# Turning the first two FFN tiles by DMA transposes of 16-bit halves instead of by TensorE

## The chip, the core and the metric

The kernel runs on one core of a Trainium2 chip. The metric is device time in microseconds (us) of one execution; less is better. The engines that matter are TensorE (PE: matmuls, with its weight loads as PEld), VectorE (DVE), ScalarE (ACT), GpSimd (POOL) and SyncE (SP), which issues the DMAs. Each engine works through its own queue of instructions in order, and semaphores make one engine wait for another. On-chip memory is SBUF; matmuls write into PSUM, which has eight banks of 128 partitions by 512 float32 values.

## The reference

One decoder layer on `x` of 256 positions by 1024 features, all float32. A mixer part (attention and a short convolution in parallel, with gates) is followed by a residual and a LayerNorm, and then by a feed-forward part (FFN) with a second residual and LayerNorm. Cut to what matters here:

```python
x = layer_norm(DEEPNORM_ALPHA * x + mix, ln1_g[l], ln1_b[l])
u = causal_dwconv(x @ w_up[l], conv_w_ffn[l])          # w_up: 1024 x 5632, three taps over positions
f = (silu(u[..., :D_FF]) * u[..., D_FF:]) @ w_down[l]  # D_FF = 2816
x = layer_norm(DEEPNORM_ALPHA * x + f, ln2_g[l], ln2_b[l])
```

The convolution runs over positions, channel by channel. It is therefore convenient to hold `x @ w_up` with the channels on the 128 partitions and the 256 positions along the free axis.

## The kernel before

**Arithmetic.** Every float32 operand of a matmul is split into a high part, rounded by a ScalarE copy to TensorE's reduced format, and a low part, which VectorE gets by subtraction. A product is the sum of high times high, high times low and low times high: three passes (`mm3`, L322), or, where the weights are the stationary side, one pass over high and low of the activations at once (`cols_wide`, L337) and one of the low weights (`cols_narrow`, L344).

**Weights.** All weights lie packed in HBM in chunks of up to 1 MB, in the order of `plan()` (L60). A chunk holds two units. SP loads the chunks in order into three rotating buffers (`raw`, `issue_dma`, L172), so the chunk after the next two can be loaded only when both units of the oldest have been split. `split_h` (L199) issues the chunk two ahead, and then makes a unit's high part on ScalarE; `split_l` (L210) makes its low part on VectorE. ScalarE's copy waits for its chunk's DMA, and everything behind it in ScalarE's queue waits with it.

**FFN.** The hidden width is cut into 22 tiles of 128 channels, each with a gate half and a value half. For tiles 2 to 21, two units (`g`, `v`) give the tile with channels on partitions in a pair of PSUM banks. Four stages follow, each with a ScalarE and a VectorE part (`FFN`, L938): stage 0 adds the two halves of the bank pair into SBUF, stage 1 applies the three convolution taps, stage 2 the silu and the product, stage 3 splits the finished tile `f` into high and low. Then `down(i)` (L978) multiplies tile i with two halves of a `w_dn` row unit, twelve passes into four PSUM banks.

**Tiles 0 and 1** are different. Their weights (`up0`) are the moving side, because `x1` for the second half of the positions comes late. `up0_rows(t)` (L950) computes 128 positions by 512 channels for t = 0 and t = 1: positions on partitions, the wrong way round. ScalarE copies the two results to SBUF (L962, L966), and eight TensorE transposes (`up0_T`, L970) turn them into two PSUM banks, one for each tile. Between the two results stand four weight splits (L963).

**Order.** The order of the work is written out by hand in `seq` (L1007): for each tile the steps `g` and `v`, and a `d` step (one `down`) for the tile three before. After step k's matmuls, `slot(k, stages)` (L1019) puts beside them: the ScalarE parts of one or two waiting tile stages, the high splits up to six steps ahead, the low splits up to five ahead, and then the VectorE parts of those stages. `take` picks the stages from `pending`, oldest first, not two of one tile. Beside a `v` step stage 0 of its tile comes first. After step 0 the transposes are issued (L1046), and the stages 1 to 3 of tiles 0 and 1 join `pending`. So tile 0's stages 1, 2 and 3 stand beside steps 0, 1 and 2, and its `down` is step 4.

The kernel already turns attention probabilities by DMA (`probs_halves`, `probs_T`, `probs_words`, L460 to L470): VectorE takes 32-bit words apart into two planes of 16-bit halves, SP issues a DMA transpose of 12 blocks of 128 by 128 halves, and ScalarE puts the words together again.

## Time and profile before

| | |
|---|---|
| time, median of 3 runs | 361.46 us (361.29 to 361.51) |
| profiled execution | 361.25 us, of which 359.5 us from the first to the last instruction |
| TensorE matmul busy | 352.1 us, 98% of the span |
| VectorE busy | 302.2 us, 84% |
| ScalarE busy | 238.9 us, 66% |
| DMA moved | 71.20 MB, mean 198 GB/s |
| mean granted TensorE clock | 0.995 |

Times in the profile count from the start of the span. A row of a group gives the line of the kernel, the engine, the operation, output and inputs by their names in the program, the shapes, the count, the busy time in us with the mean of one in ns, and the idle time of the engine just before with what ended it. A row of the timeline gives start and length in us. The chain of waits goes back from the last instruction, at each step to what released it; since matmuls are pipelined, its pieces of TensorE show the pace and not the full length of one matmul. A DMA's time to landing runs from its issue on SP to its completion.

### The profile page before, as it was taken

The page shows a single profiled execution, that of the slowest core. Times are in us where ns is not written, and L with a number is a line of the kernel's source. Part 1 is how long each engine was busy: PE and PEld are TensorE (multiplying, and loading weights), DVE is VectorE, ACT ScalarE, POOL GpSimd, SP SyncE. Part 2 cuts the span into 40 slices and gives each one's busy share as a digit, 9 for nine tenths or more (in the row PEclk, how much of TensorE's full clock was granted, in tenths as well). Part 3 has the DMA queues.
Part 4 walks back from the last instruction along what each step waited for, and adds up shares of the span by engine and source line. Part 5 has one row for each costly group of instructions (what it writes and reads, how often), then busy time and mean ns, then how long its engine had stood idle before and what let it go on. Part 6 is the DMA issues. An engine that isn't in the chain of part 4 may idle for free.

```text
span 359.5 us, 5201 instructions
## 1 busy us (share of the span) xinstructions
PE 352.1 (98%) x1915; PEld 304.3 (85%) x1915; DVE 302.2 (84%) x522; ACT 238.9 (66%) x415; POOL 22.1 (6%) x49
## 2 busy tenths in 40 slices
PE   9999999999999999999999999999999999999993
PEld 8888889888887888888888888888888888988883
DVE  4687987999888989989769789997869696999875
ACT  4586768699999976652557466766647475677800
POOL 2000001100000112310000000000000000000110
PEclk9999999999999999999999999999999999999998
DMA  8979663753955765679061736538091735663002
GB/s 284 323 263 338 221 240 122 246 168 129 261 170 174 301 228 190 216 297 339 15 233 74 277 129 224 202 148 343 19 338 59 295 127 225 233 232 120 1 33 85
DMA packets 17370, 71.20 MB, mean 198 GB/s; under 512 B 7488, under 2 KB 8000, under 8 KB 10304
## 3 DMA queue, kind: packets, MB, share of 16 engines
q1 hardware_dynamic: 16768, 68.77, 53.2%
q0 software_dynamic: 576, 2.10, 2.0%
q8 instruction: 15, 0.25, 0.3%
q14 instruction: 11, 0.09, 0.1%
HBM read 68.24 MB, written 1.05 MB: 193 GB/s over the span
## 4 chain that ended last, share of the span: by engine, by line
PE 78%; ACT 10%; DVE 7%; issue 3%; POOLq 0%; POOL 0%; DVEq 0%; ACTq 0%
PE pb L342 20%; PE pb L349 11%; PE d L324 5%; PE d L325 5%; PE d L326 4%; PE y L342 4%; PE k L614 3%; PE v L614 3%; ACT wh L203 3%; PE q L614 3%; DVE wl L213 2%; PE y L349 2%; PE o L324 2%; PE o L326 2%; PE o L325 2%
## 5 line engine op out<-in xcount | busy, mean ns | idle before, releaser
L213 DVE TENSOR_TENSOR wl<-raw,wh 128x1024 fp32r<-128x1024 f32 x99 | 121.4, 1230 | 25.3 <-ACT wh L203 25.1
L203 ACT ACTIVATE wh<-raw 128x1024 fp32r<-128x1024 f32 x99 | 103.8, 1055 | 30.5 <-DMA raw<-in_wpack 30.3
L342 PE MATMUL pb<-x1T,wh 128*128 128x512 f32 x320 | 76.2, 390 | 0.0
L342 PEld LDWEIGHTS pb<-x1T,wh 128*128 128x128 f32 x320 | 59.7, 188 | 12.1
L349 PEld LDWEIGHTS pb<-x1T,wl 128*128 128x128 f32 x320 | 41.0, 191 | 1.6
L349 PE MATMUL pb<-x1T,wl 128*128 128x256 f32 x320 | 41.5, 283 | 0.0
L342 PE MATMUL g<-xT,wh 128*128 128x512 f32 x128 | 31.6, 393 | 0.6 <-DVE gs L733 0.6
L236 DVE TENSOR_TENSOR wl<-raw,wh 128x1024 fp32r<-128x1024 f32 (+2 forms) x29 | 27.0, 974 | 5.0 <-ACT wh L235 4.8
L235 ACT ACTIVATE wh<-raw 128x1024 fp32r<-128x1024 f32 (+2 forms) x29 | 23.4, 853 | 9.8 <-DMA raw<-in_wpack 5.8
L324 PE MATMUL d<-wh,f 128*128 128x512 f32 x76 | 29.8, 392 | 0.0
L325 PE MATMUL d<-wl,f 128*128 128x512 f32 x76 | 29.8, 391 | 0.0
L326 PE MATMUL d<-wh,f 128*128 128x512 f32 x76 | 29.6, 389 | 0.0
L342 PEld LDWEIGHTS g<-xT,wh 128*128 128x128 f32 x128 | 23.2, 188 | 5.5 <-PE av L486 0.8
L902 ACT ACTIVATE fb<-pb 128x512 f32<-128x512 f32 x20 | 11.9, 595 | 13.1 <-PE pb L349 13.1
L920 DVE SCALAR_TENSOR_TENSOR fc<-fb,consts,fc 128x254 f32<-128x254 f32 x40 | 19.3, 483 | 1.4
L918 DVE SCALAR_TENSOR_TENSOR fc<-fb,consts,fc 128x255 f32<-128x255 f32 x40 | 19.2, 480 | 0.0
L912 ACT ACTIVATE fc<-fb,consts 128x256 f32<-128x256 f32 x40 | 18.0, 499 | 0.6 <-DVE fb L906 0.6
L349 PEld LDWEIGHTS g<-xT,wl 128*128 128x128 f32 x128 | 16.4, 191 | 0.7
L326 PEld LDWEIGHTS d<-wh,f 128*128 128x128 f32 x76 | 14.3, 188 | 3.1
L349 PE MATMUL g<-xT,wl 128*128 128x256 f32 x128 | 16.6, 282 | 0.0
L324 PEld LDWEIGHTS d<-wh,f 128*128 128x128 f32 x76 | 14.3, 189 | 2.6
L325 PEld LDWEIGHTS d<-wl,f 128*128 128x128 f32 x76 | 14.3, 189 | 2.4
(210 smaller groups left out, 595.4 us busy)
## 6 DMA issues: line engine op xcount, KB each, us to landing
raw<-in_wpack SPq DMA_DIRECT2D x55, 1024.0 KB, 5.0
raw<-in_wpack SPq DMA_DIRECT2D x6, 896.0 KB, 6.1
xr<-in_x SPq DMA_DIRECT2D x1, 1024.0 KB, 7.0
ln<-in_ln_g POOLq DMA_DIRECT2D x2, 512.0 KB, 5.7
ln<-in_ln_b POOLq DMA_DIRECT2D x2, 512.0 KB, 6.3
raw<-in_wpack SPq DMA_DIRECT2D x2, 384.0 KB, 4.2
raw<-in_wpack SPq DMA_DIRECT2D x2, 256.0 KB, 3.1
raw<-in_wpack SPq DMA_DIRECT2D x1, 512.0 KB, 6.0
```

The lines of the kernel that those rows point to most:

```text
L203: nc.scalar.activation(units[u]["h"], raw_of(u), AF.Copy)
L213: nc.vector.tensor_tensor(units[u]["l"], raw_of(u), units[u]["h"].bitcast(F32), op=ALU.subtract)
L235: nc.scalar.activation(h, src, AF.Copy)
L236: (eng or nc.vector).tensor_tensor(l, src, h.bitcast(F32), op=ALU.subtract)
L324: nc.tensor.matmul(o, ah, bh, start=start, stop=False)
L325: nc.tensor.matmul(o, ah, bl, start=False, stop=False)
L326: nc.tensor.matmul(o, al, bh, start=False, stop=stop)
L342: nc.tensor.matmul(bank, un["h"][:, k, n0:n0 + P], b[:, k].rearrange("p a s -> p (a s)"), start=k == 0, stop=False)
L349: nc.tensor.matmul(bank[:, 0:S], un["l"][:, k, n0:n0 + P], b[:, k, 0], start=False, stop=k == nk - 1)
L614: nc.tensor.matmul(banks[m][t], (xl if p == 2 else xh)[:, k, t * P:(t + 1) * P], wl if p == 1 else wh, start=k == 0 and p == 0, stop=k == ...
L918: nc.vector.scalar_tensor_tensor(c[:, 1:S], pb[:, a * S:a * S + S - 1], w_ffn(1, j), c[:, 1:S], op0=ALU.mult, op1=ALU.add)
L920: nc.vector.scalar_tensor_tensor(c[:, 2:S], pb[:, a * S:a * S + S - 2], w_ffn(0, j), c[:, 2:S], op0=ALU.mult, op1=ALU.add)
```

## The change

The rows of tiles 0 and 1 are no longer turned by TensorE. For each t, ScalarE copies the PSUM bank to SBUF as two planes of 16-bit halves (`up0_halves`: 128 partitions by 1024 halves), and SP issues a DMA transpose of these eight blocks. Before the first of these, the chunk that `split(u0 + 4)` would issue is issued. Beside step 2 instead of step 0, ScalarE puts the halves together again as words in SBUF (`up0_words`, two copies of 512 halves for each tile), and stages 1 to 3 of the two tiles join `pending` there. Two PSUM banks are no longer taken for tiles 0 and 1, and stages read these tiles from SBUF. The `down` steps come one tile later in `seq`, four behind instead of three, and the `w_dn` chunks one pair of chunks later in `plan()`.

```diff
@@ plan()
-        d = c - 1
+        d = c - 2
@@ layer_kernel
-    rows = {}
+    up16 = big.tile([P, 2, 2, 1024], U16, tag="x", name="up16")
...
-        rr = scratch([P, 512], f"up0r_{t}")
-        rows[t] = rr
-        return bank, rr
-
-    b0, r0 = up0_rows(0)
+        return bank
+
+    def up0_halves(t, bank):
+        nc.scalar.activation(up16[:, 0, t].rearrange("p (w n) -> p w n", w=2),
+                             bank.bitcast(U16).rearrange("p (n w) -> p w n", w=2), AF.Copy)
+        nc.sync.dma_start_transpose(up16[:, 1, t].rearrange("p (m q) -> p m q", q=P), up16[:, 0, t])
+
+    issue_dma(units[u0 + 4]["chunk"] + RAW_BUFS - 1)
+    b0 = up0_rows(0)
     x1_transpose(1, (1,))
-    nc.scalar.activation(r0, b0, AF.Copy)
+    up0_halves(0, b0)
     for v in range(4, 8):
         split(u0 + v)
-    b1, r1 = up0_rows(1)
-    nc.scalar.activation(r1, b1, AF.Copy)
-    for i in range(2):
-        PB[i] = acc_bank(f"pb{i}")
-
-    def up0_T(i):
-        for a in range(2):
-            for t in range(2):
-                nc.tensor.transpose(PB[i][:, a * S + t * P:a * S + (t + 1) * P],
-                                    rows[t][:, a * 256 + i * P:a * 256 + (i + 1) * P], ident)
+    up0_halves(1, up0_rows(1))
+
+    def up0_words(i):
+        PB[i] = scratch([P, 512], f"pb{i}")
+        for t in range(2):
+            src = up16[:, 1, t].rearrange("p (w a i q) -> p i w a q", w=2, a=2, i=2)[:, i]
+            dst = PB[i].bitcast(U16).rearrange("p (a t q w) -> p t w a q", a=2, t=2, w=2)[:, t]
+            nc.scalar.activation(dst, src, AF.Copy)
...
+    UP0_AT = 2
...
-            d = i - 3
+            d = i - 4
...
-        if k == 0:
-            up0_T(0)
-            up0_T(1)
+        if k == UP0_AT:
+            up0_words(0)
+            up0_words(1)
             pending.extend([(st, p) for p in range(2) for st in (1, 2, 3)])
```

## The prediction

> **What bounds the kernel now.** I read the page first, then the chain of waits around the first feed-forward (FFN) tiles.

> ```profile
> span 359.5 us, 5201 instructions
> PE 352.1 (98%) x1915; PEld 304.3 (85%) x1915; DVE 302.2 (84%) x522; ACT 238.9 (66%) x415; POOL 22.1 (6%) x49
> ```

> TensorE is the bound. The chain around the change says it more sharply (start, length, engine, tile, line):

> ```profile
> 180.75 0.23 PE up L326
> 180.97 1.82 PE pb L342 x8
> 182.79 0.87 PE pb L973 x8
> 183.66 1.83 PE pb L342 x8
> 185.49 1.91 PE pb L349 x16
> 187.41 3.65 PE pb L342 x16
> 191.06 1.91 PE pb L349 x16
> 192.97 0.23 PE d L324
> ```

> The pieces join end to end: TensorE waits for nobody. So each microsecond of TensorE work that disappears is a microsecond gained, and each wait put before a matmul is lost in full, because no later gap can absorb it. The eight transposes (L973) are 0.87 us. The first down matmul, D0, starts at 192.97 and needs the finished tile 0. How near is that tile? These are ScalarE's and VectorE's rows, in order of time (start, length, and in brackets the idle time before and its releaser):

> ```profile
> 176.03 0.59 ACT L962 ACTIVATE up0r<-up 128x512 f32<-128x512 f32 x1
> 176.51 3.91 ACT L235 ACTIVATE wh<-raw 128x1024 fp32r<-128x1024 f32 x4
> 181.01 0.60 ACT L966 ACTIVATE up0r<-up 128x512 f32<-128x512 f32 x1 [0.59 <-PE up L326]
> 183.26 0.84 ACT L912 ACTIVATE fc<-pb,consts 128x256 f32<-128x256 f32 x2 [1.66 <-PE pb L973]
> ...
> 187.44 0.60 ACT L902 ACTIVATE fb<-pb 128x512 f32<-128x512 f32 x1 [1.44 <-PE pb L349]
> 188.25 1.05 ACT L203 ACTIVATE wh<-raw 128x1024 fp32r<-128x1024 f32 x1
> 190.23 0.42 ACT L932 ACTIVATE f<-ff 128x256 fp32r<-128x256 f32 x1 [0.93 <-DVE ff L929]
> ```
> ```profile
> 186.23 0.48 DVE L918 SCALAR_TENSOR_TENSOR fc<-pb,consts,fc 128x255 f32<-128x255 f32 x1
> ...
> 187.65 0.48 DVE L920 SCALAR_TENSOR_TENSOR fc<-pb,consts,fc 128x254 f32<-128x254 f32 x1
> 188.04 1.22 DVE L213 TENSOR_TENSOR wl<-raw,wh 128x1024 fp32r<-128x1024 f32 x1
> 189.18 0.68 DVE L906 TENSOR_TENSOR fb<-pb,fb 128x512 f32<-128x512 f32 x1
> 189.78 0.42 DVE L929 TENSOR_TENSOR ff<-fs,fc 128x256 f32<-128x256 f32 x1
> ...
> 191.25 0.42 DVE L936 TENSOR_TENSOR f<-ff,f 128x256 fp32r<-128x256 f32 x1
> ```

> Tile 0 is ready at 191.25 + 0.42 = 191.67, 1.3 us before D0. That margin, and not the share of busy time, is what the change works on. Behind the transposes, tile 0 took 191.67 - 183.26 = 8.4 us through two engines that serve their queues in order.

> **The change, part by part.**

> *Removed:* eight transposes, -0.87 us on TensorE, for certain, and two plain copies out of PSUM (L962, L966).

> *The copies into halves.* The nearest row to a 16-bit ScalarE copy that takes 32-bit words apart or puts them together is L470:

> ```profile
> L203 ACT ACTIVATE wh<-raw 128x1024 fp32r<-128x1024 f32 x99 | 103.8, 1055 | 30.5 <-DMA raw<-in_wpack 30.3
> L470 ACT ACTIVATE sm<-halves 128x1536 uint16<-128x1536 uint16 x4 | 7.8, 1961 | 0.0
> ```

> For 1024 elements two thirds of 1961 are 1.31 us; the float row with as many elements, 1.06 us, is the lower end, 1.5 the upper. I take 1.35 each. The first starts at 176.03 and pushes the four weight splits back by 1.35 - 0.59 = 0.76 us; they end at 181.2, and the second runs from there to 182.45. Nothing on TensorE needs these splits sooner, since each is for a later unit.

> *The two DMA transposes, on SP's queue.* There they stand between weight chunks. The rows of the four transposes that the kernel has already (12 blocks each; here 8), and of chunks beside them:

> ```profile
> L466 SPq DMA_TRANSPOSE halves<-halves x1: 1541/1541/1541, 65.6 to 65.6; - x1
> DMA to landing us min/median/max: 3.8/3.8/3.8
> ...
> L179 SPq DMA_DIRECT2D raw<-in_wpack x1: 827/827/827, 67.3 to 67.3; - x1
> DMA to landing us min/median/max: 5.5/5.5/5.5
> ...
> L179 SPq DMA_DIRECT2D raw<-in_wpack x1: 333/333/333, 94.6 to 94.6; - x1
> DMA to landing us min/median/max: 5.2/5.2/5.2
> ...
> L466 SPq DMA_TRANSPOSE halves<-halves x1: 1280/1280/1280, 98.1 to 98.1; - x1
> DMA to landing us min/median/max: 3.7/3.7/3.7
> ```

> A transpose holds SP for 1.3 to 1.5 us. Behind a chunk it lands later: 98.1 + 3.7 = 101.8, two microseconds after the chunk (94.6 + 5.2 = 99.8), so some 1.3 for eight blocks. A chunk behind a transpose lands 67.3 + 5.5 - (65.6 + 3.8) = 3.4 us after it. The chunks in question today:

> ```profile
> L179 SPq DMA_DIRECT2D raw<-in_wpack x1: 328/328/328, 180.0 to 180.0; - x1
> DMA to landing us min/median/max: 4.8/4.8/4.8
> ...
> L179 SPq DMA_DIRECT2D raw<-in_wpack x1: 328/328/328, 182.3 to 182.3; - x1
> DMA to landing us min/median/max: 5.6/5.6/5.6
> ```

> The second lands at 187.9, just before ScalarE splits it at 188.25. After the change SP's order is: T0 (at 177.4, on an idle queue; it costs nothing), the first chunk at 180.0 + 0.76 = 180.75, T1 at 182.5 when the second copy ends, and only at 184.0 the next chunk, which is now the first of w_down. First chunk 180.75 + 5.0 = 185.8, T1 + 1.3 = 187.1, w_down chunk + 3.0 to 3.4 = about 190.1 to 190.5 if the queue sets it, 184.0 + 4.8 = 188.8 if it doesn't. I take 189.8, nearer to the queued case, as the rows at 65.6 to 101.8 show queueing. That is 1.9 us later than its counterpart. The chunk issued ahead of T0 keeps its place (its buffer was free long before) and costs nothing; left behind T0 it would have waited for the first copy.

> *The rows come back as words at step 2.* ScalarE's queue then reads: sum of tile 2 (waits for TensorE, 186.55), split of the first w_down unit (waits for its chunk, 189.8), then the four word copies, then tile 2's and tile 0's scalings. Everything behind the split is held by the chunk. A word copy has 512 elements: a third of 1961 is 0.65 us, 0.79 if a fifth of a microsecond is fixed, and 0.6 if it cost no more than the float copy of as many (L902); back to back each starts a tenth earlier. I take 0.7, back to back 0.6. So the split ends at 190.9 and the words at 193.3, against 183.26 + 1.82 + 3.73 = 188.8 at which a chain as in before (two TensorE steps later) would have begun.

> *The chain behind it.* Scalings of tiles 2 and 0: two times 0.84, to 194.9. VectorE: four taps for tile 2 (187.65 + 0.48 - 186.23 = 1.9 us in all) from 193.7 to 195.6, four for tile 0 to 197.5, then a weight remainder 1.22, the sum of tile 3 0.68, products of tiles 2 and 0, 0.84 together: 199.9, as each starts a tenth before the one ahead has ended (186.23 to 191.67 above shows such overlaps). ScalarE rounds tile 0 by 200.3 (0.42); VectorE's low part stands behind another remainder and tile 2's low part: 199.9 + 1.22 + 0.42 + 0.42 - 0.3 = 201.65.

> *Where D0 stands now.* One pair of up steps later and without the transposes: 192.97 - 0.87 + 3.65 + 1.91 = 197.66. It waits until 200.3 (2.65 us), runs two passes of 0.23 on the high part, and waits again from 200.75 until 201.65 (0.9). Together 3.5, with ends at 2.1 (chunk at 188.8, 1.0 less; words at 0.6, 4 × 0.1 less) and 5 (chunk at 190.5, copies at their upper ends).

> *w_down one tile later.* Chunks and steps rotate alike: step 4 and 7, 5 and 8, 6 and 9 still share a chunk, so SP's waits for buffers keep their pattern; as many instructions of each kind run. Nothing, as long as the chunks stay ahead as in the rows above; a chunk late by 1 us would be seen first as a longer idle time before L203. The two PSUM banks that tiles 0 and 1 held are free for D0's accumulators: no wait stood there (192.97 joins its predecessor), so no gain.

> **Sum.** The profiled execution took 361.25 us (span 359.5 and 1.75 around it), 0.2 less than the median 361.46. 361.25 - 0.87 + 3.5 = 363.9, and with the 0.2 to the median about 364.0: 0.7% slower.

> [...]

> **Rivals.**

> *A: full gain, 360.6.* Tile 0 keeps up and only the transposes go: 361.46 - 0.87. It decides at D0 = 197.66: for both parts of tile 0 to be there, the words must end 3.5 us sooner, near 189.8 instead of 193.3. For it: ScalarE still idles 1.44 us before L902, and T1 itself lands by about 187. Against: the split ahead of the words would need its chunk by 189.8 - 3.5 = 186.3, and issued at 182.5, with nothing ahead of it, it would land at 182.5 + 4.8 = 187.3. It is not slower than before: the other side.

> *B: no measurable change, 362.0.* T1 slips into gaps between packets and the w_down chunk lands at 187.9 as its counterpart did. Then everything behind the split moves 1.9 us ahead, and of 3.5 us of stall 1.6 stay: 361.46 - 0.87 + 1.6 = 362.2; with word copies at 0.6 it is 361.8. I put it between, at 362.0, just inside what can be told from no change. Against it: SP cannot issue the chunk while it issues T1, and the row at 98.1 shows transposes queueing.

> *C: the clock falls, about 365.6.* An idle TensorE may be given a lower clock for a while after the stall:

> ```profile
> 354.00:359.50 5.50, 0.00 (x0) 0.00 (x0) 2.07 (x5) 0.00 (x0) 0.55 (x1) 0.70 0.27 95
> ```

> In the last stretch TensorE is idle (0.00 busy) and its granted clock averages 0.70, a loss of 0.30 × 5.5 = 1.65 us of clock. As much lost behind the stall gives 364.0 + 1.65. Against: the stall is split by two passes, and shorter than 5.5 us. [...]

> **How the numbers follow.** Stall at D0 with the clock kept: 0.58, alone 362.7 to 365.6. C, or a chunk still later: 0.12. B: 0.17. A: 0.13. A measurement of this kernel can tell about 0.2%, 0.7 us, from no change: A alone is faster (0.13), B is the same (0.17), the rest slower (0.70). The range, 360.5 to 365.8, takes in A and nearly all of C, because leaving A out would already spend most of the two in ten.

> **What would show it.** Right: in the chain of waits D0 (the first d L324) no longer joins its predecessor; TensorE idles about 2.7 us there with ScalarE's rounding of f as releaser, and about 0.9 us more two passes later with VectorE's; the first w_down chunk is issued near 184 and lands near 190; a word copy takes 0.65 to 0.8 us; ScalarE's split at that place waits 2.5 to 3 us for its chunk. Wrong: a chain of TensorE without a gap at D0, or the words done before 190, means A; a gap under 1.5 us means B; a gap before other steps than D0 means that the rotated chunk order is not neutral.

## The result and the profile after

The changed kernel takes 366.27 us (median of 6 runs, 365.07 to 367.17) against 361.49 us before (361.29 to 363.04): a ratio of 1.0123, 95% interval 1.0096 to 1.0149. It is slower, as forecast, but by more than the forecast 364.0, and above the range's upper end of 365.8. The profiled execution took 366.93 us, the second slowest of the six, with a span of 365.2. From its page, the first lines and the row of granted TensorE clock (40 slices of the span, in tenths):

```profile
span 365.2 us, 5191 instructions
PE 354.4 (97%) x1907; PEld 305.5 (84%) x1907; DVE 302.7 (83%) x522; ACT 241.5 (66%) x419; POOL 22.2 (6%) x49
...
PEclk9999999999999999999999699999999999999999
```

Eight matmuls fewer, and yet TensorE's busy time has grown by 2.3 us: some of its instructions became slower, and the clock row has a dent in the slice that begins at 201 us. The chain of waits around the first FFN tiles, in the form shown of before (start, length, engine, tile, line):

```profile
183.37 6.98 DMA raw<-in_wpack
...
190.44 1.06 ACT wh L203
191.50 2.56 ACT pb L976 x4
194.06 0.36 ACT fc L912
...
201.74 0.68 DVE f L936 x2
202.42 0.04 issue
202.46 0.79 PE d L326
203.25 0.43 PE d L324
...
206.67 0.38 PE d L326
207.05 3.65 PE pb L342 x16
```

Where the chain ran through TensorE alone, it now leaves it: from the DMA of the first w_down chunk (issued at 183.37, landed 6.98 us later) through the split, the four word copies (L976) and VectorE's stages of tiles 2 and 0 to the first down matmul, D0. Then each pass of D0 takes 0.43 us where it took 0.23. ScalarE's rows show the queue that does it (start, length, in brackets the idle time before and its releaser):

```profile
180.99 1.02 ACT L959 ACTIVATE up<-up 128x1024 uint16<-128x1024 uint16 x1 [0.17 <-PE up L326]
181.91 1.05 ACT L203 ACTIVATE wh<-raw 128x1024 fp32r<-128x1024 f32 x1
185.44 1.06 ACT L203 ACTIVATE wh<-raw 128x1024 fp32r<-128x1024 f32 x1 [2.47 <-DMA raw<-in_wpack]
186.53 0.60 ACT L902 ACTIVATE fb<-pb 128x512 f32<-128x512 f32 x1
190.44 1.06 ACT L203 ACTIVATE wh<-raw 128x1024 fp32r<-128x1024 f32 x1 [3.31 <-DMA raw<-in_wpack]
191.41 2.66 ACT L976 ACTIVATE pb<-up 128x512 uint16<-128x512 uint16 x4
```

The second transpose had landed long before the words were put together. These rows are its issue on SP and its time to landing, 182.0 + 4.3 = 186.3 us:

```profile
L961 SPq DMA_TRANSPOSE up<-up x1: 1238/1238/1238, 182.0 to 182.0; - x1
...
DMA to landing us min/median/max: 4.3/4.3/4.3
```

So for five microseconds, to 191.41, the turned halves lay in SBUF while ScalarE did the sum of tile 2 (0.60 us), idled for 3.31 us in front of a split whose weights had not come, and split them (1.06 us). What TensorE lost can be read from the waits between 176 and 203 us and from three stretches (length; then busy time of PE, PEld, DVE, ACT and POOL with their counts, the granted clock, the DMA's share and GB/s):

```profile
PE d L324 <- ACT f L932: 3.5, 1, 3.5
...
PEld d L326 <- DVE f L936: 0.9, 1, 0.9
```
```profile
196.62:200.04 3.42, 1.01 (x9) 0.80 (x7) 3.35 (x7) 2.10 (x4) 0.00 (x0) 1.00 0.00 0
200.04:203.45 3.41, 2.21 (x4) 1.33 (x5) 3.41 (x6) 2.98 (x6) 0.00 (x0) 0.50 0.85 310
203.45:206.86 3.41, 3.41 (x9) 2.64 (x8) 3.34 (x7) 2.46 (x5) 0.00 (x0) 0.50 1.01 384
```

TensorE waits 3.5 us for the high part of tile 0, its weight load waits 0.9 us for the low part, and from 200.04 to 206.86 it has half its clock. With the full clock the ten passes after the second wait would have taken, by estimate, 0.50 us for the first (the pass behind the wait took so long in the run with TensorE kept busy, its row stands below) and 9 × 0.23 for the others, from 202.46 to 205.03; they end at 207.05, so the clock cost 2.0 us. Together -0.87 + 4.4 + 2.0 = 5.5 us, against 365.2 - 359.5 = 5.7 us of span; the 0.2 left are about what the first pass behind the wait takes longer.

### The profile page after: what moved, and what is told of

Its sections match the earlier page's. It is cut to its first block, busy times and chain, and to the rows that moved or that the text cites. A ratio compares the mean times of both kernels' runs of the same rounds, so it can differ in the third digit from the quotient of the medians.

```text
span 365.2 us, 5191 instructions
## 1 busy us (share of the span) xinstructions
PE 354.4 (97%) x1907; PEld 305.5 (84%) x1907; DVE 302.7 (83%) x522; ACT 241.5 (66%) x419; POOL 22.2 (6%) x49
## 3 DMA queue, kind: packets, MB, share of 16 engines
HBM read 68.24 MB, written 1.05 MB: 190 GB/s over the span
## 4 chain that ended last, share of the span: by engine, by line
PE 87%; DVE 4%; issue 3%; DMA 2%; ACT 2%; POOLq 0%; POOL 0%; DVEq 0%; SPq 0%; ACTq 0%
PE pb L342 17%; PE pb L349 9%; PE g L342 7%; PE d L326 5%; PE d L324 5%; PE d L325 5%; PE y L342 4%; PE g L349 4%; PE k L614 3%; PE v L614 3%; PE q L614 3%; PE b L342 2%; PE y L349 2%; PE c L342 2%; PE o L325 2%
## 5 line engine op out<-in xcount | busy, mean ns | idle before, releaser
L213 DVE TENSOR_TENSOR wl<-raw,wh 128x1024 fp32r<-128x1024 f32 x99 | 121.7, 1232 | 20.4 <-ACT wh L203 17.8
L203 ACT ACTIVATE wh<-raw 128x1024 fp32r<-128x1024 f32 x99 | 103.6, 1052 | 23.8 <-DMA raw<-in_wpack 23.7
L342 PE MATMUL pb<-x1T,wh 128*128 128x512 f32 x320 | 75.9, 389 | 0.0
L342 PEld LDWEIGHTS pb<-x1T,wh 128*128 128x128 f32 x320 | 59.9, 188 | 12.3
L349 PEld LDWEIGHTS pb<-x1T,wl 128*128 128x128 f32 x320 | 41.0, 191 | 1.6
L349 PE MATMUL pb<-x1T,wl 128*128 128x256 f32 x320 | 41.5, 283 | 0.0
L324 PE MATMUL d<-wh,f 128*128 128x512 f32 x76 | 30.9, 406 | 3.5 <-ACT f L932 3.5
L342 PE MATMUL g<-xT,wh 128*128 128x512 f32 x128 | 31.4, 393 | 0.4 <-DVE gs L733 0.4
L326 PE MATMUL d<-wh,f 128*128 128x512 f32 x76 | 30.6, 403 | 0.1
L325 PE MATMUL d<-wl,f 128*128 128x512 f32 x76 | 30.7, 404 | 0.0
L235 ACT ACTIVATE wh<-raw 128x1024 fp32r<-128x1024 f32 (+2 forms) x29 | 23.4, 852 | 9.5 <-DMA raw<-in_wpack 5.5
L342 PEld LDWEIGHTS g<-xT,wh 128*128 128x128 f32 x128 | 23.2, 188 | 5.2 <-PE av L486 0.7
L902 ACT ACTIVATE fb<-pb 128x512 f32<-128x512 f32 x20 | 11.8, 592 | 23.8 <-PE pb L349 23.8
L906 DVE TENSOR_TENSOR fb<-pb,fb 128x512 f32<-128x512 f32 x20 | 13.8, 688 | 8.2 <-ACT fb L902 8.1
L918 DVE SCALAR_TENSOR_TENSOR fc<-fb,consts,fc 128x255 f32<-128x255 f32 x40 | 19.2, 479 | 1.7 <-ACT fc L912 1.7
L920 DVE SCALAR_TENSOR_TENSOR fc<-fb,consts,fc 128x254 f32<-128x254 f32 x40 | 19.4, 484 | 1.4
L324 PEld LDWEIGHTS d<-wh,f 128*128 128x128 f32 x76 | 14.9, 195 | 6.3 <-ACT f L932 3.7
L912 ACT ACTIVATE fc<-fb,consts 128x256 f32<-128x256 f32 x40 | 17.9, 497 | 1.3 <-DVE fb L906 1.3
L326 PEld LDWEIGHTS d<-wh,f 128*128 128x128 f32 x76 | 14.8, 195 | 4.1 <-DVE f L936 0.9
L349 PEld LDWEIGHTS g<-xT,wl 128*128 128x128 f32 x128 | 16.4, 191 | 0.7
```

The lines of the kernel that those rows point to most:

```text
L203: nc.scalar.activation(units[u]["h"], raw_of(u), AF.Copy)
L213: nc.vector.tensor_tensor(units[u]["l"], raw_of(u), units[u]["h"].bitcast(F32), op=ALU.subtract)
L235: nc.scalar.activation(h, src, AF.Copy)
L324: nc.tensor.matmul(o, ah, bh, start=start, stop=False)
L325: nc.tensor.matmul(o, ah, bl, start=False, stop=False)
L326: nc.tensor.matmul(o, al, bh, start=False, stop=stop)
```

## The experiments

The theory is that the words stand, in ScalarE's queue, behind a split that waits for a weight chunk, that the second transpose on SP's queue delays this chunk, and that the clock falls because TensorE waits. The rivals are that the DMA transposes are too slow for their place (1), that the later place of w_down costs (2), that the DMA traffic or another engine is at fault (3), and that the words' place alone counts (4). All times are medians, beside runs of the kernel before on the same chip (361.24 to 361.28 us).

### Words one step earlier

```diff
-    UP0_AT = 2
+    UP0_AT = 1
```

> The changed kernel with the words put together beside step 1 instead of step 2, so that in ScalarE's queue they stand ahead of the split that waits for the first w_down chunk. Theory (queue order: the words stand behind a split that waits for a late chunk): the words end near 189.1 instead of 194.06 us, the second transpose having landed at 186.35; tile 0 is ready well before 197.5 us, the chain of TensorE has no gap at the first down matmul, the granted clock stays 1.00, and only the eight transposes are gone: 360.6 us (361.49 - 0.87). Rival 1 (the DMA transposes themselves are too slow for this place): the words still end after 190 us, a gap of more than 1 us stays at the first down matmul, 362 us or more. Rival 2 (the later place of w_down costs): no gap at the first down matmul, but the time stays above 362 us.

360.16 us (359.86 to 360.72), ratio to before 0.9969, interval 0.9957 to 0.9981: faster than both kernels. The word copies now stand ahead of the waiting split:

```profile
186.53 2.64 ACT L976 ACTIVATE pb<-up 128x512 uint16<-128x512 uint16 x4
190.30 1.05 ACT L203 ACTIVATE wh<-raw 128x1024 fp32r<-128x1024 f32 x1
```

and the chain of waits is TensorE's alone again, D0 joining its predecessor at 195.78 + 1.91 = 197.69:

```profile
195.78 1.91 PE pb L349 x16
197.69 0.23 PE d L324
197.92 0.23 PE d L325
198.16 0.23 PE d L326
```

The chunk was nearly as late here (issued 183.4, 6.7 us to landing), behind the same two transposes; the words, and behind them stages 1 to 3 of the two tiles, stand one step earlier in the queues, and that is all that differs. This rules out rivals 1 and 2 as the cause.

### TensorE kept busy while it waits

```diff
         else:
+            if i == 0:
+                for _ in range(14):
+                    nc.tensor.matmul(dacc[1][1], x1T[:, 0, 0, 0:P], x1T[:, 0].rearrange("p a s -> p (a s)"), start=True, stop=True)
             down(i)
```

> The changed kernel with 14 matmuls of 512 columns (0.23 us each, 3.2 us in all) ahead of the first down matmul, into a bank that this one then starts anew: their results are thrown away. They fill most of the 3.5 us for which TensorE stood idle. Theory (the clock falls because TensorE idles): the first down matmul starts when tile 0 is ready, as before near 201.1 us of the span, but the granted clock between 200 and 208 us stays near 1.00 instead of 0.50 and 0.64, its twelve passes take 2.75 us plus the second wait of about 0.9 instead of 6, and the time is about 2.1 us less than the changed kernel's 366.27: 364.1 us, with less spread between runs. Rival (the slow passes have another cause, such as contention for PSUM or SBUF with the other engines): the passes still take 0.43 us each and the time stays near 366.3 us or is above it.

364.71 us (363.99 to 364.82), ratio 1.0095, interval 1.0080 to 1.0109. Its spread is 0.8 us where the changed kernel's is 2.1. The same stretches:

```profile
196.62:200.03 3.41, 3.41 (x21) 2.96 (x20) 3.38 (x7) 1.86 (x5) 0.00 (x0) 1.00 0.23 34
200.03:203.45 3.42, 3.17 (x15) 2.30 (x14) 3.42 (x6) 2.43 (x6) 0.00 (x0) 1.00 0.94 383
203.45:206.86 3.41, 3.41 (x17) 2.83 (x16) 3.34 (x7) 2.46 (x5) 0.00 (x0) 1.00 0.97 339
```
```profile
201.49 0.50 PE d L326
```

The clock stays at 1.00 beside the same traffic (383 and 339 GB/s against 310 and 384), so traffic isn't what slows the passes. 361.28 - 0.87 + 4.4 = 364.8 is the changed kernel's wait without the clock, and 364.71 was measured: the wait is the larger part of the loss and the clock some 1.6 us of the median. The match of the two is in part chance, since the chunk's landing varies: in this profiled execution, the fastest of the four (363.99 us), it came at 183.3 + 6.0 = 189.3, and the third pass of D0, the first that needs the low part, at 201.49 instead of 202.46. So of the 2.9 us between the two profiled executions one is the earlier chunk's, and the clock's are 2.0, as worked out above.

### The later w_down alone

```diff
 # in the kernel before
-        d = c - 1
+        d = c - 2
...
-            d = i - 3
+            d = i - 4
```

> The kernel before, with its TensorE transposes, with only the w_down steps one tile later and their chunks one pair of chunks later. Theory (this part is neutral, all loss comes from the words' place): 361.5 us, no gap in the chain of TensorE, chunk waits of ScalarE no longer than before in total (30 us). Rival 2 (the rotated order of chunks costs by itself): 362.5 us or more, with a gap of TensorE at some step.

361.55 us (360.86 to 362.00), ratio 1.0003, interval 0.9994 to 1.0011: nothing. D0 joins its predecessor (197.22 + 1.91 = 199.13), and the transposes are still there:

```profile
183.37 0.87 PE pb L973 x8
...
197.22 1.91 PE pb L349 x16
199.13 0.23 PE d L324
```

Rival 2 falls a second time.

### The w_down chunk ahead of the second transpose

```diff
+    issue_dma(units[u0 + 4]["chunk"] + RAW_BUFS + 1)
     up0_halves(1, up0_rows(1))
```

> The changed kernel with the first w_down chunk issued ahead of the second DMA transpose instead of behind it. Theory (this transpose on SP's queue makes the chunk late, and with it everything behind its split): the chunk is issued near 182.6 us and lands near 187.9 instead of 190.36; the second transpose then lands near 189.5 and sets the words, which end near 192.1 instead of 194.06; the wait at the first down matmul falls from 4.4 to about 2.5 us, too short for the clock to fall: 363.1 us. Rival 1 (the transposes are too slow for this place wherever they are issued): behind the chunk the second one lands after 191 us, and the time stays above 365 us. Rival 3 (the chunk's delay comes from slow DMA traffic and not from its place): it lands after 189.5 us all the same.

364.15 us (362.81 to 364.89), ratio 1.0071, interval 1.0053 to 1.0090. The chunk came at 182.9 + 6.0 = 188.9, one microsecond later than expected, and its split starts there:

```profile
189.03 1.06 ACT L203 ACTIVATE wh<-raw 128x1024 fp32r<-128x1024 f32 x1 [1.65 <-DMA raw<-in_wpack]
190.00 2.67 ACT L977 ACTIVATE pb<-up 128x512 uint16<-128x512 uint16 x4
```
```profile
196.73:200.15 3.42, 1.59 (x12) 1.24 (x10) 3.42 (x6) 1.87 (x4) 0.00 (x0) 1.00 0.29 77
200.15:203.56 3.41, 2.93 (x8) 2.02 (x7) 3.37 (x7) 2.49 (x5) 0.00 (x0) 0.50 1.01 420
```

The second transpose, now behind the chunk (which held SP from 182.93 for 0.33 us), landed at most 6.7 us after its issue: the words, which need it, start without a wait at 190.00, when the split ends. The two changed places on SP's queue, and behind this split the words could not start sooner. They start 1.4 us earlier than in the changed kernel, and TensorE idles 1.83 + 0.48 = 2.3 us instead of 3.6 in such stretches. The direction is the theory's; the size isn't: I expected the clock to hold, and in this execution it fell for one stretch of 3.4 us; that 2.5 us would be too short for a fall was an estimate of mine that no run shows, and here it fell behind a wait of 1.8. Where it held, the forecast of 363.1 was near: two of the six runs took 362.8 us with a mean granted clock of 0.996 and 0.998, the others 363.9 to 364.9 with 0.992 to 0.994. The chunk missed rival 3's 189.5 by only 0.6 us.

### No DMA transposes at all

```diff
-        nc.sync.dma_start_transpose(up16[:, 1, t].rearrange("p (m q) -> p m q", q=P), up16[:, 0, t])
...
-            src = up16[:, 1, t].rearrange("p (w a i q) -> p i w a q", w=2, a=2, i=2)[:, i]
+            src = up16[:, 0, t].rearrange("p (w a i q) -> p i w a q", w=2, a=2, i=2)[:, i]
```

> The changed kernel without its two DMA transposes: the words are put together from the halves as they are, so tiles 0 and 1 are not turned and this part of the computation is left out; all copies stay at their places. It shows what is left of the loss when SP's queue is free. Theory (the second transpose delays the first w_down chunk by some 2.5 us, and the words' place behind the split of this chunk costs the rest): the chunk is issued near 182.6 us and lands near 187.9, the words end near 191.5 instead of 194.06, a wait of about 1.9 us stays at the first down matmul, and the time is about 362.3 us, or up to 1 us more if the clock still falls. Rival 1 (the transposes are the whole cause): no gap at the first down matmul and 360.4 us. Rival 4 (the place of the words alone is the cause, whatever SP does): the gap stays near 4 us and the time above 365 us.

363.52 us (361.85 to 365.45), ratio 1.0065, interval 1.0039 to 1.0091. The chunk was issued at 183.3 and landed after 5.1 us, at 188.4, two microseconds before the changed kernel's. Landings vary: issued behind the second transpose, a chunk took 6.0 to 7.2 us in the six kernels here that have one in this place, and without transposes 5.1 us here and 5.5 us in the next run, so the transposes' share is by estimate between 0.5 and 2 us. Even so TensorE waits, in two pieces:

```profile
PE d L324 <- ACT f L932: 0.9, 1, 0.9
PE d L326 <- DVE f L936: 0.6, 1, 0.6
```
```profile
197.72:201.14 3.42, 1.93 (x10) 1.21 (x9) 3.42 (x7) 2.81 (x6) 0.00 (x0) 1.00 0.77 268
201.14:204.55 3.41, 3.41 (x10) 2.63 (x9) 3.34 (x7) 2.41 (x5) 0.00 (x0) 0.50 1.01 420
```

Neither rival 1 (no gap) nor rival 4 (the whole gap) holds: in this execution words at step 2 cost a wait of 1.5 us with a free SP queue, and with the transposes it was 4.4 in the changed kernel's. I had expected a wait of 1.9 us and up to 1 us more for the clock; the wait was shorter, and the clock still fell for a whole stretch.

### The same with TensorE kept busy

The same kernel with the extra matmuls of the second experiment, 4 instead of 14.

> The kernel without the two DMA transposes (tiles 0 and 1 not turned, this part of the computation left out), and with 4 matmuls of 512 columns (0.9 us) whose results are thrown away ahead of the first down matmul. Theory (a wait of 0.9 and 0.6 us there costs its own length, and the clock's fall, which comes or not by how the wait lies in the clock's windows of 3.4 us, makes the rest and the wide spread of the run without them): only the second wait of 0.6 us is idle, the granted clock stays 1.00 from 200 to 208 us, the first down matmul's place is the same, and the time is 361.24 - 0.87 + 1.6 = 362.0 us, with a spread well under the 3.6 us seen without the extra matmuls. Rival 3 (the spread comes from the landing of the chunks): the time stays near 363.5 us with a spread of some 3 us.

362.68 us (361.94 to 363.38), ratio 1.0036, interval 1.0022 to 1.0050, with the clock at 1.00. The spread falls from 3.6 to 1.4 us, and the median by 0.8. That is the theory's direction, while 0.7 us more than expected remain. The waits of this execution are 0.4 and 0.6 us behind 0.9 us of extra matmuls, 1.9 together. Behind the second wait a pass takes 0.50 us instead of 0.23 (at 200.11), and by estimate the one behind the first too: 361.25 - 0.87 + 1.9 + 0.5 = 362.8, which is the measured time to 0.1 us. That the whole of the spread without the extra matmuls comes from the clock is not shown.

### Down steps two tiles later

```diff
-            d = i - 4
+            d = i - 5
```

> The changed kernel with the down steps five tiles behind instead of four (the order of the chunks in memory as changed). The unit split ahead of the words is then one of a chunk that has landed long before, and the first down matmul stands 5.6 us of TensorE later. Theory: the words end near 190.5 us, tile 0 is ready long before its down matmul, no gap in the chain of TensorE, 360.4 us. Rival 2 (a later w_down costs by itself, in the buffers or at the end): a gap or a longer end, over 361.3 us.

360.26 us (359.84 to 360.59), ratio 0.9972, interval 0.9962 to 0.9981: the full gain by another way. The words (188.13 to 190.79) stand behind a unit whose chunk has been there for long, and D0 joins its predecessor:

```profile
201.31 1.91 PE pb L349 x16
203.22 0.23 PE d L324
```

### Words at step 1, w_down at its old place

```diff
 # on the words at step 1
-        d = c - 2
+        d = c - 1
...
-            d = i - 4
+            d = i - 3
```

> The changed kernel with the words at step 1 and with w_down back at its old place (three tiles behind, chunks as before). Theory (the time from the second transpose to a finished tile 0 needs the later place of w_down): the words end near 189.2 us as with the words at step 1 alone, the high part of tile 0 is ready near 194.3, but the first down matmul stands at 192.1: it waits 2.2 us and then about 0.9 more for the low part, the clock falls for a while, and the time is 363.5 to 364.5 us. Rival (the step of the words alone decides): no gap at the first down matmul and 360.4 us, so that the later w_down was not needed.

367.48 us (367.39 to 367.66), ratio 1.0175, interval 1.0162 to 1.0189, slower than the change itself. So the DMA path does need the later w_down; my figure was 3 us too low. The first wait is as worked out (2.1 us for 2.2), the second much longer (2.5 us for 0.9), and the clock stays low for two stretches:

```profile
PE d L326 <- DVE f L936: 2.5, 1, 2.5
PE d L324 <- ACT f L932: 2.1, 1, 2.1
```
```profile
192.28:195.70 3.42, 0.73 (x2) 0.30 (x2) 3.35 (x7) 3.42 (x7) 0.00 (x0) 1.00 0.00 0
195.70:199.11 3.41, 1.86 (x4) 1.50 (x5) 3.37 (x7) 1.67 (x3) 0.00 (x0) 0.50 0.53 144
199.11:202.52 3.41, 3.41 (x9) 2.65 (x8) 3.11 (x6) 1.06 (x2) 0.00 (x0) 0.50 1.02 428
```

361.24 - 0.87 + 4.6 = 365.0 is the wait. Of the remaining 2.5 us the clock cost an estimated 2.1: the ten passes from 197.25 end at 201.89, and with the full clock 0.50 + 9 × 0.23 would have ended them at 199.82. For the low part I had left out that VectorE does the remainder of a weight unit and a tile's sum ahead of it.

### No chunk ahead of the first transpose

```diff
 # on the words at step 1
-    issue_dma(units[u0 + 4]["chunk"] + RAW_BUFS - 1)
```

> The changed kernel with the words at step 1 and without the line that issues the next weight chunk ahead of the first DMA transpose, so that this chunk stands behind it on SP's queue. Theory (SP holds the chunk until the first copy into halves is done): the chunk is issued near 178.8 us instead of 166.4 and lands near 183.7, where ScalarE would have split its first unit at 182; the later chunks land 1 to 1.5 us later, the words end 1 to 2 us later than 189.2, and tile 0 still has its margin: no gap at the first down matmul, 360.2 us, the same as with the line. Rival (the line is needed): a gap opens at step 2 or at the first down matmul and the time is 361.5 us or more.

362.45 us (361.51 to 362.91), ratio 1.0032, interval 1.0021 to 1.0044. The rival is right: the line is worth 2.3 us. The profiled execution, the fastest of these (361.51), has the words end at 190.66, as late as expected, but tile 0's low part then comes too late:

```profile
PE d L326 <- DVE f L936: 0.8, 1, 0.8
```
```profile
197.02:200.43 3.41, 2.57 (x15) 1.92 (x14) 3.41 (x6) 2.24 (x5) 0.00 (x0) 1.00 0.41 91
200.43:203.84 3.41, 3.41 (x17) 2.81 (x16) 3.34 (x7) 1.41 (x3) 0.00 (x0) 1.00 1.02 406
```

What the slower of these runs lose beyond 0.8 us was not profiled; their mean granted clock, 0.995 to 0.999, is no lower than that of the quickest two, 0.995 and 0.997, so the clock is not seen to be the reason.

## Why the prediction was right and wrong

**Right: the bound and the place.** TensorE without a gap meant that the transposes' 0.87 us is the whole gain, and it is there as soon as nothing waits (360.16 and 360.26 us, 1.0 to 1.1 us under before with some 0.4 us of uncertainty; rival A's sum was 0.87 under). D0's place without a wait was 197.66 in the prediction, and 197.69 in the kernel with the words at step 1. The two waits at D0, ScalarE's and then VectorE's, and the chain from the w_down chunk to them came as forecast.

**Right in kind, off in size: the wait.** 4.4 us instead of 3.5. The copies into halves took 1.02 us, not 1.35, so the second transpose left at 182.0 (182.5 forecast) and landed at 186.3 (187.1), and SP issued the chunk at 183.37 (184.0). All of this was faster, and still the chunk landed at 190.36 instead of 189.8: it came 4.0 us behind the transpose, where I had 3.0 to 3.4 from one earlier row and, with 189.8, took 2.7. That the error is only 0.56 us is luck: the transpose's early landing hid the other 0.7. The words ended at 194.06 (193.3), 0.56 us of it the chunk, the rest word copies of 0.76 us (0.63 back to back) for my 0.7 and 0.6. Behind the words the sum held: high part at 201.05, low part at 202.41, both 0.75 us after the forecast times.

**Wrong: the clock.** The step that failed is the argument against rival C, that the wait is split by two passes and shorter than the 5.5 us of its row, so that the sum had no term for the clock. C was given 0.12 together with a still later chunk, and 1.65 us; it came, with 2.0 us in the profiled execution and 1.3 to 1.6 us of the medians (366.27 against the wait's 365.0 here, and against 364.71 with TensorE kept busy). Its size was near, and its chance was far too small: the clock fell at 200.04, before the two passes between the waits, at the end of a step of 3.41 us with 2.41 us of idle time, and without the transposes it fell behind a step with 1.49 us (last section). A wait of 4.4 us alone gives 361.49 - 0.87 + 4.4 = 365.0, inside the range; the clock took the median to 366.27 and outside.

**The edits costed at nothing.** The later w_down is neutral by itself, as said (1.0003), and I didn't say that the words at step 1 without it would be slower still (367.48). The chunk ahead of the first transpose keeps its place, as said; that its absence costs 2.3 us with the words at step 1 is more than the wait for one copy that I named. The freed PSUM banks were not tried alone.

**The transposes' price.** A DMA transpose of eight blocks landed after 3.1 us on the idle queue, 4.3 us when issued 1.6 us behind a chunk and at most 6.7 us when it came straight behind one. The kernel before already had a row of the last kind, which the prediction left out: its third transpose of twelve blocks, issued at 88.87 and 0.4 us behind a chunk, held SP for 2.24 us and landed after 7.1, where the other three landed after 3.7 to 3.8.

## To carry to other kernels

When work moves from a full engine to a DMA, look at what stands ahead of its consumer in an in-order queue: here a split that waited for a weight chunk cost five times what the transposes had, and one step earlier in the same queue it cost nothing. A DMA on SP's queue delayed the one close behind it here, a chunk behind a transpose by an estimated 0.5 to 2 us, and a transpose behind a chunk by 1.2 us (4.3 against 3.1) and, in the kernel before, 3.4 us (7.1 against 3.7), so name the next one and who waits for it. Where TensorE has no gaps, price a new gap at its length, and read the granted clock behind it: here it was halved behind 1.49 us and more of idle time in a step of 3.41 us, and the spell cost an estimated 2 us in the changed kernel.

## What the runs showed of the hardware

**The granted clock.** In these executions it changed in steps of 3.41 us, counted from its first record in a run: in the changed kernel it fell 57 steps after 5.48 us, at 200.04, rose two steps later, at 206.86, and fell again 46 steps later, at 363.88; in the kernel before it fell at 356.20, 103 steps after 4.63. The stretches shown above lie on these steps. TensorE's idle time in one stretch, its length less PE's busy time, goes with the clock of the next:

| kernel | idle us in the stretch | clock of the next |
|---|---|---|
| without transposes | 1.49 | 0.50 |
| chunk ahead of the second transpose | 1.83, then 0.48 | 0.50, then 1.00 |
| changed | 2.41, then 1.20 | 0.50, then 0.50 |
| words at step 1, old w_down | 2.69, then 1.55 | 0.50, then 0.50 |
| no chunk ahead | 0.84 | 1.00 |
| without transposes, TensorE kept busy | at most 0.99 | 1.00 |
| changed, near its end | 1.26, then 3.42 | 1.00, then 0.50 |
| without transposes, near its end | 1.37 | 1.00 |
| TensorE kept busy | 0.00, then 0.25 | 1.00 |

The two rows near the end are these, of the changed kernel and of the one without transposes:

```profile
357.05:360.46 3.41, 2.15 (x18) 1.95 (x17) 3.05 (x10) 0.00 (x0) 0.41 (x1) 1.00 0.00 0
360.46:363.88 3.42, 0.00 (x0) 0.00 (x0) 1.55 (x3) 0.00 (x0) 0.14 (x1) 1.00 0.44 153
```
```profile
354.74:358.15 3.41, 2.04 (x18) 1.83 (x16) 2.96 (x9) 0.00 (x0) 0.53 (x1) 1.00 0.00 0
```

**Sixteen-bit copies on ScalarE.** Taking words apart, from PSUM into two planes of halves, ran at the float pace (1.02 us for 1024 halves against 1.06 us for 1024 floats). Putting them together, with halves written next to each other as words, took 0.76 us for 512, against 0.60 us for 512 floats.
